# Norming row tiles one by one at the end of an output projection, with a longer tail for one stream

## The chip, the cores and the metric

The kernel runs on one core of a Trainium2 chip. The metric is the device time of one execution in microseconds (us). TensorE does the matmuls, VectorE (DVE) and ScalarE (ACT) the work on rows and columns, GpSimd (POOL) a few small operations, and SyncE (SP) issues most transfers from HBM.

## The reference

Two blocks run one after the other on 256 tokens of width 1024; the change is in the second. This has two layers, and it carries two streams, the latent tokens x and the context tokens xc, 256 tokens each. Each layer has three sub-layers: a feed-forward network, a mix of attentions and a Fourier transform, and another feed-forward network. In each of them the rows are normed and modulated, go through the sub-layer, and its output is normed and added back:

```python
def ffn_sublayer(h, m, sub, g_pre, g_post, w1, w2):
    shift, scale, gate = mods_of(m, sub)
    y = swiglu(modulate(rms_norm(h, g_pre[sub]), shift, scale), w1, w2)
    return h + MACARON_WEIGHT * gate * rms_norm(y, g_post[sub])
...
    o = jnp.concatenate([o_a, o_b, o_c], axis=-1) @ w_out
    x = x + gt * rms_norm(o, g_post[1])
    x = ffn_sublayer(x, mod, 2, g_pre, g_post, w_ffn_in[1], w_ffn_out[1])
```

In the last layer the context stream ends with the attention's keys and values: the last output projection of an attention and the last feed-forward network work on x alone.

## The kernel before

All matmuls run as three products of float32 parts: a matrix is split into a high half `h` (a cast on ScalarE, L175) and a low half `l` (a subtraction on VectorE, L176), and h·h, h·l and l·h are added up in PSUM. `wload` does it for weights: a transfer of 128 x 1024 into `wr` (4 buffers), then the split into `wh` and `wl` (3 buffers each).

`out_proj` (L1366 on) is the last step of every sub-layer: the product with the output weights, the norm of its rows, and the addition to `X[s][t]`. Rows come in tiles of 128: `t` is 0 or 1 within stream `s`. So `n` is 4 with two streams and 2 with one. The width of 1024 is done in two halves, `c` = 0 and 1. For each half the loop over weight tiles `u` does both or all four row tiles with each weight tile, but holds the last two weight tiles back (`rest`). With them the row tiles are completed two at a time and one after the other, so that the work on a finished tile runs beside the matmuls of the next one. With four tiles, part of an earlier weight tile is held back for tiles 2 and 3 as well (`split`).

The work on a finished row tile `i` of half 1: a Square on ScalarE whose sum is kept (L1411), the product with the gate into `tmp` (L1417, VectorE), the sum of the squares of both halves (L1419), a power of -1/2 on GpSimd (`rsqrt`, L204), and two updates of x, half by half (L1424).

If a sub-layer follows (`nxt`), its first step stands in here. `rows(s, t)` norms a tile's rows: two squares on ScalarE (L1326), their sum (L1328), a power on GpSimd, and one scaling (L1331) into `xn`. `cols(s)` then turns the normed rows of both tiles of a stream with 16 transposes on TensorE (L170), applies shift and scale on ScalarE (L1347) and splits the result into `hh` and `hl` on VectorE (L1350, L1351). Before, `rows` for both tiles of a stream follows the update of its second tile. With one stream `cols` comes right behind; with two, `cols(0)` is written behind the matmuls of tiles 2 and 3, and `cols(1)` is called by the next sub-layer's `first_units`, which also loads that sub-layer's first weights. With one stream all of these but the first are queued behind the first operations of `cols` (`issue_after`).

Five calls of `out_proj` have a `nxt`: the two feed-forward networks and the attention of layer 0 and the first feed-forward network of layer 1 with two streams, and the attention of layer 1 with one. The last feed-forward network has none. In layer 0 a generator (`mods_rows`) computes later modulations on VectorE in the background (L1188), a piece per weight load.

The order of the instructions on each engine is made by a scheduler, which takes what its own model of the times has ready, and of that what is written first. An engine then runs its instructions in that fixed order.

Of the kernel before, what the change touches and what calls it, by code (L numbers as in the profile page):

```python
# [157 lines left out]
class Build:  # L158
# [1207 lines left out]
    def out_proj(self, l, sub, streams, w, KT, lhs, weight, nxt, spare, yo=None, ahead=None):  # L1366

        nc = self.nc
        V, A, G = nc.vector, nc.scalar, nc.gpsimd
        g = self.gate(l, sub, streams)  # L1370
        tiles = [(s, t) for s in streams for t in range(2)]
        n, KU = len(tiles), KT // 2
        yo = self.yout() if yo is None else yo
        y = [spare[:, 0], spare[:, 1], yo[:, 0], yo[:, 1]]
        sq = self.us.tile([128, 2, 4], F32, name="sq", bufs=2)

        def load(u, *pool):
            h, lo = ahead.pop(0) if ahead else self.wload(w[:, 1024 * u : 1024 * u + 1024], 1024)
            return [(h[:, 512 * k :], lo[:, 512 * k :]) + lhs(2 * (u % KU) + k, *pool) for k in range(2)]

        def product(ps, i, k, parts):
            o = 256 * tiles[i][0] + 128 * tiles[i][1]
            h, lo, a, b = parts
            self.move(ps[i], h, lo, 1, k, KT, lambda _: (a[:, o : o + 128], b[:, o : o + 128]))

        for c in range(2):

            ps = [self.acc() if (c == 0 and i < 2) or (c and n == 4 and i) else self.bank() for i in range(n)]
            split = c and nxt and n == 4
            for u in range(KU - 2):  # L1390
                early = split and u == KU - 3
                parts = load(c * KU + u, *((self.pt, "pt", "pt") if early else ()))
                for k in range(2):
                    for i in range(2 if early else n):
                        product(ps, i, 2 * u + k, parts[k])

            rest = [p for u in range(KU - 2, KU) for p in load(c * KU + u)]
            if c and nxt:
                self.pre(*nxt)
            for i, (s, t) in enumerate(tiles):  # L1400
                if t == 0:
                    if split and s:
                        for k in range(2):
                            for j in (i, i + 1):
                                product(ps, j, KT - 6 + k, parts[k])
                    for j in (i, i + 1):
                        for k, r in enumerate(rest):
                            product(ps, j, KT - 4 + k, r)
                    if c and nxt and s:
                        self.cols(0)  # L1410
                A.activation(self.junk(), ps[i], AF.Square, accum_out=sq[:, c, i : i + 1])  # L1411
                half = slice(512 * c, 512 * c + 512)
                if c == 0:
                    V.tensor_tensor(out=y[i], in0=ps[i], in1=g[:, s, half], op=ALU.mult)
                    continue
                tmp = self.u2.tile([128, 512], F32, name="u2")
                V.tensor_tensor(out=tmp, in0=ps[i], in1=g[:, s, half], op=ALU.mult)  # L1417
                rs = self.us.tile([128, 1], F32, name="rso")
                V.scalar_tensor_tensor(out=rs, in0=sq[:, 0, i : i + 1], scalar=D * RMS_EPS, in1=sq[:, 1, i : i + 1],  # L1419
                                       op0=ALU.add, op1=ALU.add)  # L1420
                self.rsqrt(rs, rs, 1)
                for c2, part in enumerate((y[i], tmp)):
                    x = self.X[s][t][:, 512 * c2 : 512 * c2 + 512]
                    V.scalar_tensor_tensor(out=x, in0=part, scalar=rs, in1=x, op0=ALU.mult, op1=ALU.add)  # L1424
                if nxt and t:
                    for t2 in range(2):
                        self.rows(s, t2)
                    if n == 2:
                        self.cols(s)

    def first_units(self, n, streams, src):
# [403 lines left out]
```

## Time and profile before

| | |
|---|---|
| time, median of 3 runs | 2624.18 us (2622.79 to 2625.65) |
| the profiled execution | 2622.96 us |
| its span | 2621.1 us |
| TensorE matmuls busy | 2530.6 us (97%), 16658 instructions |
| VectorE busy | 1753.0 us (67%) |
| ScalarE busy | 1132.1 us (43%) |
| GpSimd busy | 183.7 us (7%) |
| read from HBM | 379.80 MB, 146 GB/s over the span |

A busy time is the sum over an engine's instructions. The span runs from the first to the last instruction of the profiled execution; the device time has 1.86 us around it. In the page's slices TensorE is busy to 90% or more in all but the first and the last.

### The profile page before, as it was taken

The page shows a single profiled execution, that of the slowest core. Times are in us where ns is not written, and L with a number is a line of the kernel's source. Part 1 is how long each engine was busy: PE and PEld are TensorE (multiplying, and loading weights), DVE is VectorE, ACT ScalarE, POOL GpSimd, SP SyncE. Part 2 cuts the span into 40 slices and gives each one's busy share as a digit, 9 for nine tenths or more (in the row PEclk, how much of TensorE's full clock was granted, in tenths as well). Part 3 has the DMA queues.
Part 4 walks back from the last instruction along what each step waited for, and adds up shares of the span by engine and source line. Part 5 has one row for each costly group of instructions (what it writes and reads, how often), then busy time and mean ns, then how long its engine had stood idle before and what let it go on. Part 6 is the DMA issues. An engine that isn't in the chain of part 4 may idle for free.

```text
span 2621.1 us, 42324 instructions
## 1 busy us (share of the span) xinstructions
PE 2530.6 (97%) x16658; PEld 2158.3 (82%) x16658; DVE 1753.0 (67%) x3102; ACT 1132.1 (43%) x1936; POOL 183.7 (7%) x219
## 2 busy tenths in 40 slices
PE   8999999999999999999999999999999999999998
PEld 7888999877899888887866778887788888866897
DVE  6988567797766785567777475556664445655656
ACT  5365445444545432233546342223432224555545
POOL 1121100112100000000112010000000000011000
PEclk9999999999999999999999999999999999999999
DMA  6334466545537564445441244444445543322565
GB/s 201 108 117 138 131 202 213 164 146 186 161 115 217 190 203 149 152 141 158 136 123 55 89 145 153 153 153 137 149 156 153 153 137 97 105 89 80 171 194 152
DMA packets 124711, 384.82 MB, mean 147 GB/s; under 512 B 28352, under 2 KB 32176, under 8 KB 124384
## 3 DMA queue, kind: packets, MB, share of 16 engines
q1 hardware_dynamic: 121504, 380.19, 47.3%
q8 instruction: 131, 2.15, 0.3%
q10 hardware_dynamic: 3008, 1.92, 0.2%
q14 instruction: 68, 0.56, 0.1%
HBM read 379.80 MB, written 2.26 MB: 146 GB/s over the span
## 4 chain that ended last, share of the span: by engine, by line
PE 74%; DVE 13%; DMA 6%; issue 4%; ACT 2%; POOL 1%; DVEq 0%; POOLq 0%; SPq 0%; ACTq 0%
PE ac L167 38%; PE rw L167 22%; PE sm L167 9%; DMA wr<-in_wmodT 5%; DVE wl L176 4%; PE md L167 3%; PE sm L170 2%; DVE br L816 2%; DVE prod L1188 1%; DMA wr<-in_win 1%; ACT wh L175 1%; POOL rs L204 1%; DVE blk L1351 0%; DVE br L1424 0%; PE rw L170 0%
## 5 line engine op out<-in xcount | busy, mean ns | idle before, releaser
L175 ACT CAST wh<-wr 128x1024 fp32r<-128x1024 f32 (+2 forms) x547 | 569.3, 1042 | 850.2 <-PE ac L167 375.8
L176 DVE TENSOR_TENSOR wl<-wr,wh 128x1024 fp32r<-128x1024 f32 (+2 forms) x547 | 665.1, 1217 | 239.4 <-ACT wh L175 233.9
L1188 DVE CUSTOM_DVE_ANT_0 prod<-wr,cr 128x1024 f32<-128x1024 f32 x208 | 254.4, 1223 | 305.8 <-DMA wr<-in_wmodT 304.7
L167 PE MATMUL rw<-blk,wh 128*128 128x512 f32 (+1 forms) x1600 | 423.3, 350 | 5.3 <-DVE blk L1350 4.7
L167 PE MATMUL ac<-blk,wh 128*128 128x512 f32 (+1 forms) x1552 | 410.4, 350 | 2.6 <-DVE blk L1350 1.8
L167 PE MATMUL ac<-xth,wh 128*128 128x256 f32 x1248 | 357.5, 287 | 7.2 <-ACT wh L175 5.2
L167 PE MATMUL ac<-xth,wl 128*128 128x256 f32 x1248 | 351.0, 281 | 2.7 <-DVE wl L176 2.6
L167 PE MATMUL ac<-xtl,wh 128*128 128x256 f32 x1248 | 350.0, 281 | 0.1
L167 PEld LDWEIGHTS rw<-blk,wh 128*128 128x128 f32 x1600 | 283.0, 189 | 46.5 <-DVE blk L1350 5.6
L167 PEld LDWEIGHTS ac<-blk,wh 128*128 128x128 f32 x1552 | 274.2, 189 | 42.2 <-DVE blk L1350 2.3
L167 PE MATMUL rw<-blk,wl 128*128 128x512 f32 (+1 forms) x800 | 279.2, 349 | 2.2 <-DVE wl L176 2.2
L167 PE MATMUL ac<-blk,wl 128*128 128x512 f32 (+1 forms) x776 | 271.0, 349 | 2.0 <-DVE wl L176 2.0
L167 PEld LDWEIGHTS ac<-xth,wh 128*128 128x128 f32 x1248 | 236.9, 190 | 17.7 <-issue 7.3
L167 PEld LDWEIGHTS ac<-xth,wl 128*128 128x128 f32 x1248 | 236.4, 190 | 6.1 <-DVE wl L176 4.7
L167 PEld LDWEIGHTS ac<-xtl,wh 128*128 128x128 f32 x1248 | 236.6, 190 | 2.5 <-issue 1.5
L175 ACT CAST ah<-blk 128x512 fp32r<-128x512 f32 (+1 forms) x170 | 95.8, 566 | 194.1 <-PE sm L167 99.7
L167 PEld LDWEIGHTS rw<-blk,wl 128*128 128x128 f32 x800 | 151.2, 189 | 22.4 <-DVE wl L176 3.1
L167 PEld LDWEIGHTS ac<-blk,wl 128*128 128x128 f32 x776 | 146.9, 189 | 21.7 <-DVE wl L176 2.6
L176 DVE TENSOR_TENSOR al<-blk,ah 128x512 fp32r<-128x512 f32 (+1 forms) x170 | 104.0, 620 | 62.2 <-ACT ah L175 62.0
L816 DVE SCALAR_TENSOR_TENSOR br<-hp,pv,br 128x256 f32<-128x256 f32 x240 | 114.1, 511 | 0.9
L167 PE MATMUL ac<-f,wh 128*128 128x256 f32 x640 | 114.1, 281 | 0.0
L167 PEld LDWEIGHTS ac<-f,wh 128*128 128x128 f32 x640 | 97.1, 188 | 1.1 <-issue 0.6
(440 smaller groups left out, 4136.9 us busy)
## 6 DMA issues: line engine op xcount, KB each, us to landing
wr<-in_w SPq DMA_DIRECT2D x264, 512.0 KB
wr<-in_win SPq DMA_DIRECT2D x187, 512.0 KB
wr<-in_wmodT SPq DMA_DIRECT2D x120, 512.0 KB
wr<-in_wo SPq DMA_DIRECT2D x32, 512.0 KB
wr<-in_wout SPq DMA_DIRECT2D x32, 512.0 KB
wr<-in_wmod SPq DMA_DIRECT2D x24, 512.0 KB
wr<-in_wkv SPq DMA_DIRECT2D x16, 512.0 KB
gate<-gd SPq DMA_DIRECT2D x10, 512.0 KB
```

Of the source, the lines that this page charges most:

```text
L167: self.nc.tensor.matmul(out, a, b, start=start, stop=stop, skip_group_check=True)
L170: self.nc.tensor.transpose(out, a, self.ident[:n, :n])
L175: nc.scalar.copy(h, src)
L176: (eng or nc.vector).tensor_tensor(out=l, in0=src, in1=h.bitcast(F32), op=ALU.subtract)
L204: self.nc.gpsimd.tensor_tensor(out=out, in0=in_, in1=self.mhalf[:p, :n], op=ALU.pow)
L816: V.scalar_tensor_tensor(out=acc, in0=hp[:, j : j + 256], scalar=w(j), in1=acc, op0=ALU.mult, op1=ALU.add)
L1188: V.tensor_tensor_reduce(out=self.prod, in0=raw, in1=self.cr[:, r], scale=1.0, scalar=0.0, op0=ALU.mult, op1=ALU.add, accum_out=m[:, g, r ...
```

## The change

With `nxt`, `rows` for a tile now follows that tile's own update, ahead of the work on the next tile, and no longer waits for the second tile of its stream. And with one stream, in the second half of the width, three weight tiles are held back instead of two, so that the two row tiles are completed with 18 matmuls each, one after the other, instead of 12. Nothing else changes: the same instructions on the same data.

```diff
--- before.py
+++ after.py
@@ -1387,14 +1387,16 @@
 
             ps = [self.acc() if (c == 0 and i < 2) or (c and n == 4 and i) else self.bank() for i in range(n)]
             split = c and nxt and n == 4
-            for u in range(KU - 2):
+
+            tail = 3 if c and nxt and n == 2 else 2
+            for u in range(KU - tail):
                 early = split and u == KU - 3
                 parts = load(c * KU + u, *((self.pt, "pt", "pt") if early else ()))
                 for k in range(2):
                     for i in range(2 if early else n):
                         product(ps, i, 2 * u + k, parts[k])
 
-            rest = [p for u in range(KU - 2, KU) for p in load(c * KU + u)]
+            rest = [p for u in range(KU - tail, KU) for p in load(c * KU + u)]
             if c and nxt:
                 self.pre(*nxt)
             for i, (s, t) in enumerate(tiles):
@@ -1405,7 +1407,7 @@
                                 product(ps, j, KT - 6 + k, parts[k])
                     for j in (i, i + 1):
                         for k, r in enumerate(rest):
-                            product(ps, j, KT - 4 + k, r)
+                            product(ps, j, KT - 2 * tail + k, r)
                     if c and nxt and s:
                         self.cols(0)
                 A.activation(self.junk(), ps[i], AF.Square, accum_out=sq[:, c, i : i + 1])
@@ -1422,10 +1424,9 @@
                 for c2, part in enumerate((y[i], tmp)):
                     x = self.X[s][t][:, 512 * c2 : 512 * c2 + 512]
                     V.scalar_tensor_tensor(out=x, in0=part, scalar=rs, in1=x, op0=ALU.mult, op1=ALU.add)
-                if nxt and t:
-                    for t2 in range(2):
-                        self.rows(s, t2)
-                    if n == 2:
+                if nxt:
+                    self.rows(s, t)
+                    if n == 2 and t:
                         self.cols(s)
 
     def first_units(self, n, streams, src):
```

## Rows read from the trace of the kernel before

**Rows 1.** Busy time by stage; columns: window, length, engines (instructions), clock, DMA share, GB/s.

```profile
1265.00:1298.00 33.00, 28.90 (x168) 24.95 (x166) 25.90 (x51) 17.02 (x40) 6.65 (x8) 0.95 0.43 118
1500.00:1535.00 35.00, 29.70 (x180) 25.36 (x179) 27.35 (x54) 18.45 (x43) 9.44 (x8) 1.00 0.43 136
1881.00:1914.00 33.00, 27.66 (x175) 23.91 (x174) 25.54 (x52) 18.86 (x43) 6.26 (x8) 1.00 0.40 127
2252.00:2285.00 33.00, 30.70 (x190) 27.23 (x189) 25.15 (x50) 18.76 (x43) 4.70 (x8) 0.95 0.36 91
2418.00:2440.00 22.00, 15.82 (x91) 13.54 (x91) 14.40 (x27) 12.28 (x25) 2.21 (x4) 0.84 0.37 118
```

**Rows 2.** Timeline, TensorE, one-stream end: start, duration, instruction, [idle before <-releaser].

```profile
2429.45 0.87 PE L170 MATMUL sm<-ident,u 128*128 128x128 f32 x3 [5.33 <-DVE rs L1328]
```

**Rows 3.** Chain that ended last, one-stream end: start, length, engine and line.

```profile
2413.24 8.18 PE sm L167 x36
...
2421.49 0.70 ACT junk L1411 x2
...
2426.40 1.42 DVE br L1424 x2
...
2428.55 0.75 DVE u L1331
...
2430.03 0.76 DVE u L1331
```

**Rows 4.** Timeline, ScalarE, one-stream end.

```profile
2418.71 1.05 ACT L175 CAST wh<-wr 128x1024 fp32r<-128x1024 f32 x1 [1.67 <-PE sm L167]
...
2424.21 0.60 ACT L1411 ACTIVATE junk<-sm 128x512 bf16<-128x512 f32 x1 [2.03 <-PE sm L167]
...
2427.25 0.63 ACT L1326 ACTIVATE junk<-br 128x512 bf16<-128x512 f32 x1 [0.84 <-DVE br L1424]
...
2428.54 0.19 ACT L1326 ACTIVATION_READ_ACCUMULATOR junk<-br 128x1 f32 x1
```

**Rows 5.** Timeline, VectorE, one-stream end.

```profile
2417.08 1.23 DVE L176 TENSOR_TENSOR wl<-wr,wh 128x1024 fp32r<-128x1024 f32 x1 [0.85 <-ACT wh L175]
...
2423.66 0.75 DVE L1424 SCALAR_TENSOR_TENSOR br<-blk,rso,br 128x512 f32<-128x512 f32 x1 [0.69 <-POOL rso L204]
```

**Rows 6.** Timeline, VectorE, third two-stream end.

```profile
1889.33 0.15 DVE L1328 SCALAR_TENSOR_TENSOR rs<-ss 128x1 f32<-128x1 f32 x1
1890.21 0.75 DVE L1331 TENSOR_SCALAR u<-br,rs 128x1024 f32<-128x1024 f32 x1 [0.73 <-POOL rs L204]
1890.88 1.22 DVE L176 TENSOR_TENSOR wl<-wr,wh 128x1024 fp32r<-128x1024 f32 x1
...
1892.89 0.75 DVE L1331 TENSOR_SCALAR u<-br,rs 128x1024 f32<-128x1024 f32 x1 [0.73 <-POOL rs L204]
```

**Rows 7.** Timeline, TensorE, first, second and fourth two-stream ends.

```profile
1280.34 1.64 PE L170 MATMUL sm<-ident,u 128*128 128x128 f32 x13 [1.61 <-DVE u L1331]
...
1516.20 1.65 PE L170 MATMUL sm<-ident,u 128*128 128x128 f32 x13 [1.15 <-DVE u L1331]
...
2267.72 0.39 PE L167 MATMUL rw<-blk,wh 128*128 128x256 f32 x1 [1.67 <-DVE blk L1350]
```

**Rows 8.** Timeline, TensorE, second half of the third end.

```profile
1905.87 0.38 PE L167 MATMUL ac<-blk,wl 128*128 128x256 f32 x1 [1.37 <-DVE wl L176]
```

**Rows 9.** Busy time in 2 us of the fourth end.

```profile
2270.00:2272.00 2.00, 2.00 (x11) 2.00 (x11) 2.00 (x7) 0.56 (x1) 0.00 (x0) 0.50 0.46 105
```

**Rows 10.** Timeline, ScalarE, third end.

```profile
1884.16 0.60 ACT L1411 ACTIVATE junk<-rw 128x512 bf16<-128x512 f32 x1 [2.09 <-PE rw L167]
...
1887.33 0.19 ACT L1326 ACTIVATION_READ_ACCUMULATOR junk<-br 128x1 f32 x1
```

**Rows 11.** Timeline, GpSimd, second and third end.

```profile
1512.41 1.46 POOL L204 TENSOR_TENSOR rs<-rs,mhalf 128x1 f32<-128x1 f32 x1 [1.60 <-DVE rs L1328]
...
1889.62 0.55 POOL L204 TENSOR_TENSOR rs<-rs,mhalf 128x1 f32<-128x1 f32 x1 [1.66 <-DVE rs L1328]
```

## The prediction

> **What bounds the kernel now.** I read the page first: TensorE is busy for 97% of the span, so a change that adds no arithmetic can only win back TensorE's idle time. Then I made a table by stage around the five places where this change acts, the ends of the output projections that norm rows for a next sub-layer. Four have two streams (four row tiles); one, in the last attention, has one stream (two tiles) [rows 1]. In these windows TensorE is idle for 4.1, 5.3, 5.3, 2.3 and 6.2 us (window less busy time), together 23.2 us or 0.9% of the span. That is the ceiling, and part of it belongs to the casts behind the norm, which stay.
>
> TensorE's timeline at the one-stream end shows one gap of 5.33 us, which ends when rows are normed [rows 2]. The chain of waits leads through it: ScalarE's square of the finished product, VectorE's product with the gate, a power on GpSimd, two updates of x, two squares; then, for each tile, a one-column sum, a power and the scaling [rows 3]. The two scalings start at 2428.55 and 2430.03, since tile 1's sum stands in VectorE's queue behind tile 0's scaling. That is what the change takes apart.
>
> **The change part by part.** No instruction is added or removed. In the one-stream tail 18 matmuls of each tile instead of 12 are done tile by tile, rows() moves up by one tile, and no DMA moves with it.
>
> *The one-stream end (once).* 36 matmuls of this tail take 8.18 us, 0.227 us each [rows 3]. With three held weight tiles, six more matmuls of tile 1 stand behind tile 0, so tile 0's product is complete 6 x 0.227 = 1.36 us earlier, and its Square moves from 2421.49 to about 2420.13. Tile 1 completes as before, its Square ready to run at 2424.21 [rows 4]. Tile 0's updates move from 2423.66 [rows 5] to 2422.30 and end at 2423.72 (1.42 us, [rows 3]). Its two squares then run from about 2423.15 to 2424.63: such a pair takes 1.48 us, as from 2427.25 to 2428.73 [rows 4]. They are written ahead of tile 1's Square now, which thus starts at 2424.63 and not at 2424.21: 0.42 us lost. Gained is that tile 1's sum no longer waits for tile 0's scaling, which ends at 2429.30 [rows 3]; its squares are read at 2428.73, so at most 0.57 us. The two nearly cancel: I take -0.1 us, with bounds -0.57 (tile 1's Square goes first) and +0.42 (only the loss stays). The gap of 5.33 us is a chain of tile 1 alone, from its own Square on, and more cover for tile 0 does not shorten that.
>
> The third held tile has two costs that I put at nothing. The last weight's low half is ready at 2417.08 + 1.23 = 2418.31 [rows 5]. Tile 0's 18 matmuls then end at 2413.24 + 8.18 - 1.36 = 2420.06 [rows 3], so they start some 0.2 us (the way of the last result) over 4.09 us earlier, at about 2415.8, and want this half after 13 of them, at about 2418.75. The cover is 0.4 us; without it TensorE stalls by what is missing, and tile 1's Square comes as much later. And the next sub-layer's first weight, whose cast now runs at 2418.71 in a free place of the weight buffer [rows 4], must wait until tile 1 has used the first held tile, to about 2421.3. Its cast (1.05 us) fits into ScalarE's pause before tile 0's squares, its split (1.23 us) into VectorE's pause after tile 0's updates (2423.7 to 2425), and it is needed only past the transposes, after 2431. Behind them are queued the squares of tile 0 and the gate product of tile 1, at most 0.4 us late. With this the bounds are -0.6 and +0.8 us.
>
> *The two-stream ends (four).* The products don't change here; only rows() moves. In VectorE's timeline of the third one, tile 0's sum follows tile 1's updates at 1889.33, the scaling starts 0.88 us later, at 1890.21, after 0.73 us of idle time, the next instruction at 1890.88, and tile 1's scaling at 1892.89 [rows 6]. Tile 0's norm thus takes 0.88 + 0.67 = 1.55 us of the queue between tile 1's updates and tile 1's sum. Moved up, its own work (0.07 + 0.67) still lies ahead of tile 1's last update, but the wait for its power is covered by tile 1's power and first update. Saved: 1.55 - 0.74 = 0.81 us per end. Does TensorE get it? In the first three ends it waits for a scaling, by 1.61 us in the first and 1.15 in the second, the least; in all four it then waits for a cast, by 1.67 us in the fourth [rows 7], and the casts stand in the same queue of VectorE behind the same waits. So I take 0.8 us each, -3.2 us in all. Bounds per end: 0 (a cast keeps its place behind a weight split that needs the same time) and -1.6 (tile 1's round trip to GpSimd is filled with other work too).
>
> *The second half of these ends (tiles 2 and 3).* Tile 2's norm moves ahead of tile 3's updates. TensorE doesn't wait for it there, but waits 1.37 us for a weight split in the third end [rows 8]; a scaling of 0.75 us put ahead of such a split would lengthen that. I take 0, with bounds -0.6 and +0.75 in three ends, +2.2 us.
>
> *The clock.* The granted clock is 0.50 (1.2 GHz) for a while after TensorE's idle stretch in the fourth end [rows 9]; the windows of the first and fourth ends average 0.95, those of the second and third, with more idle time, 1.00 and 1.00 [rows 1]. A mean of 0.95 over 33 us is 3.3 us at half speed, a loss of 1.65 us. A shift can take that away at two ends or bring it to two others: 0 taken, bounds -3.3 and +3.3.
>
> Sum: -0.1 - 3.2 = -3.3 us. The profiled execution, 2622.96 us (span 2621.1 and 1.86 around it), would become 2619.7; it lies 1.2 us under the median of 2624.18, against which I forecast 2624.18 - 3.3 = 2620.9 us.
>
> **The rivals.**
> *Written order in the queues, slower.* If ScalarE takes tile 0's two squares ahead of tile 1's Square at the two-stream ends too, that Square waits for tile 0's updates. In the third end tile 0's squares are read at 1887.52, and the Square that ran at 1884.16 starts then [rows 10]; tile 1's gate product comes behind tile 0's scaling, at 1887.52 + 0.88 + 0.67 = 1889.1. From there: 1.47 to the update (2422.19 to 2423.66), 1.42 for both, 0.91 until their squares are read (2427.82 to 2428.73), 0.88 and 0.75 [rows 3 to 6], so tile 1 is normed at 1894.5 instead of 1893.64: 0.9 us late, and 2.1 if the weight split of 1.22 us in that stretch still stands there. At the one-stream end the gate product starts at 2426.2 instead of 2425.08 (2423.66 + 1.42), less the 0.57: +0.6. In all +4.2 to +9.0, about 2631 us. It decides wherever tile 1's product is complete before tile 0's squares are done, so at all five ends. Against it: the trace is not in written order. The next sub-layer's first cast, written behind the whole projection, runs ahead of its last squares [rows 4], so what is ready goes first.
>
> *A stretched power, no change.* The power takes 0.55 us where VectorE idles for it, and 1.46 us where a weight split runs beside it [rows 11]. After the change VectorE works beside tile 0's power. If tile 1's are hit as well, 0.91 us per end are given back, more than the 0.81 gained: +0.4 - 0.1 us in all, 2624.5 us. For it speaks that a split is beside a power in the second end already; against it, that tile 1's powers keep their neighbours. The Trainium skill, "SBUF — State Buffer", section "Who interferes with whom", says that a VectorE instruction with two SBUF inputs and a GpSimd one that reads SBUF block each other for a whole instruction. By that rule a change that fills VectorE's waits pays with longer powers; the two rows agree with it.
>
> *A larger gain.* Both round trips are filled, and the clock stays up at the first and fourth ends: -6.4 - 0.1 - 3.3 = -9.8 us at most, about 2616 us with half of the clock's part. For it: waits of over 1.1 us for a scaling at three ends [rows 7]; against it, that the casts stay in the same queue.
>
> **How the numbers follow.** Forecast, -1 to -5.2 us: 0.58. No change, by stretched powers or because the casts keep their place: 0.17. Larger gain: 0.16. Written order: 0.09. 0.2% is 5.2 us, about what a measurement of this kernel can tell from no change. The forecast, but for a tail of 0.04 below, and the no-change case lie within it, the larger gain beyond it, written order beyond it in two cases of three: faster 0.20, same 0.74, slower 0.06. The range reaches into the larger gain, down to 2615.5, and over the no-change case with the bounds of the second halves, up to 2626.5; most of the slower rival and a tail of the larger gain stay outside.
>
> **What would show it.** Right: at the one-stream end tile 0's Square 4.1 to 4.5 us ahead of tile 1's instead of 2.7, and the gap still near 5 us; at the two-stream ends tile 0's scaling ahead of tile 1's last update, and waits for a scaling shorter by some 0.8 us. Wrong: tile 1's Square behind tile 0's squares at the two-stream ends (written order); powers over 1 us in tile 1's chain (stretched); the last weight late, as a wait of TensorE for a split inside the one-stream tail; a gap well under 5 us there, which would mean that I missed what sets it.

## The result: 0.57% slower

| | before | after |
|---|---|---|
| time, median of 5 runs on one chip | 2625.65 us (2622.79 to 2631.76) | 2643.23 us (2635.35 to 2644.3) |
| ratio, 95% interval | | 1.0057 (1.0034 to 1.008) |
| the profiled execution | 2622.96 us | 2641.94 us |
| its span | 2621.1 us | 2640.1 us |
| mean granted clock of TensorE | 0.992 | 0.984 |

The forecast was 3.3 us less, within 2615.5 to 2626.5. The ratio, which is not the quotient of the two medians (1.0067), says some 15 us more, with an interval of about 9 to 21 us. The sign was wrong and the range missed the time.

Of the profiled execution after the change, the page's busy times:

```profile
PE 2541.4 (96%) x16658; PEld 2175.0 (82%) x16658; DVE 1754.6 (66%) x3102; ACT 1133.8 (43%) x1936; POOL 180.0 (7%) x219
```

The number of matmuls is the same, and VectorE and ScalarE work as long as before. TensorE is busy 10.8 us longer (2530.6 before) and idle 8.2 us longer (span less busy time: 90.5 before, 98.7 now). Both show in one group of instructions, the transposes of `cols`; its idle time grows by more than the whole, since other waits fall away (those for the casts of `cols`, 6.5 us before). Columns: busy us, mean ns | idle just before them, and what ended it. First after, then before.

```profile
L170 PE MATMUL sm<-ident,u 128*128 128x128 f32 x416 | 73.7, 315 | 38.7 <-DVE u L1331 33.6
```

```profile
L170 PE MATMUL sm<-ident,u 128*128 128x128 f32 x416 | 65.1, 288 | 19.5 <-DVE u L1331 11.5 <-DVE rs L1328 5.3 <-ACT u L1347 1.3
```

TensorE now waits 33.6 us for scalings of rows (L1331) instead of 16.8 (11.5 + 5.3), and the same transposes take 8.6 us longer, since the clock is lower when they run.

**Where it happens: the order of two queues.** In the code after, the Square of `out_proj` is L1413, the gate product L1419, the updates of x L1426; `rows` keeps its lines. ScalarE's timeline in the third two-stream end, after, answers [rows 10]:

```profile
1890.63 0.60 ACT L1413 ACTIVATE junk<-sm 128x512 bf16<-128x512 f32 x1 [4.09 <-PE sm L167]
...
1894.97 0.63 ACT L1326 ACTIVATE junk<-br 128x512 bf16<-128x512 f32 x1 [3.65 <-DVE br L1426]
...
1895.72 0.63 ACT L1326 ACTIVATE junk<-br 128x512 bf16<-128x512 f32 x1
...
1896.48 0.60 ACT L1413 ACTIVATE junk<-rw 128x512 bf16<-128x512 f32 x1
```

Tile 1's Square (`rw`) follows tile 0's (`sm`) by 5.85 us. Before it followed by 2.78 us (1881.38 below and 1884.16, [rows 10]), when TensorE finished the product. Now it stands behind tile 0's two squares of `rows`. ScalarE idles 3.65 us ahead of these, though tile 1's product is ready from about 1893.4 on (2.78 us after tile 0's Square). The second half has the same order, and there it costs more. ScalarE before, then after:

```profile
1881.38 0.60 ACT L1411 ACTIVATE junk<-sm 128x512 bf16<-128x512 f32 x1 [4.09 <-PE sm L167]
...
1892.33 0.60 ACT L1411 ACTIVATE junk<-rw 128x512 bf16<-128x512 f32 x1 [0.36 <-PE rw L167]
```

```profile
1912.11 0.63 ACT L1326 ACTIVATE junk<-xc 128x512 bf16<-128x512 f32 x1 [2.13 <-DVE xc L1426]
...
1913.63 0.60 ACT L1413 ACTIVATE junk<-rw 128x512 bf16<-128x512 f32 x1
```

Before, tile 3's Square ran when its product was done (1892.33). After, TensorE starts the last matmul of that product at 1901.08, and the Square comes at 1913.63, some 12 us later: it stands behind tile 2's two squares, and these behind tile 2's updates, which VectorE does only after the casts of `cols(0)`. VectorE in the third end, after (answers [rows 6]):

```profile
1896.48 0.16 DVE L1328 SCALAR_TENSOR_TENSOR rs<-ss 128x1 f32<-128x1 f32 x1 [0.94 <-ACT junk L1326]
1897.37 0.75 DVE L1331 TENSOR_SCALAR u<-br,rs 128x1024 f32<-128x1024 f32 x1 [0.73 <-POOL rs L204]
1898.04 0.68 DVE L1419 TENSOR_TENSOR u<-rw,gate 128x512 f32<-128x512 f32 x1
...
1903.60 0.75 DVE L1331 TENSOR_SCALAR u<-br,rs 128x1024 f32<-128x1024 f32 x1 [0.73 <-POOL rs L204]
...
1914.67 0.75 DVE L1331 TENSOR_SCALAR u<-xc,rs 128x1024 f32<-128x1024 f32 x1 [0.73 <-POOL rs L204]
1915.34 0.68 DVE L1419 TENSOR_TENSOR u<-rw,gate 128x512 f32<-128x512 f32 x1
...
1920.18 0.75 DVE L1331 TENSOR_SCALAR u<-xc,rs 128x1024 f32<-128x1024 f32 x1 [0.56 <-POOL rs L204]
```

Tile 1's gate product starts only when tile 0 has been scaled (1898.04 behind 1897.37), and in the second half tile 3's behind tile 2's (1915.34 behind 1914.67). The two tiles of a stream are now worked on one after the other, round trips to ScalarE and GpSimd included, where before they overlapped: from tile 2's scaling to tile 3's it takes 5.51 us, before 1.55 us. TensorE's timeline, after, second halves of the four two-stream ends (tiles 2 and 3):

```profile
1300.71 2.61 PE L170 MATMUL sm<-ident,u 128*128 128x128 f32 x11 [3.58 <-DVE u L1331]
...
1537.67 3.03 PE L170 MATMUL sm<-ident,u 128*128 128x128 f32 x13 [4.56 <-DVE u L1331]
...
1920.99 2.10 PE L170 MATMUL sm<-ident,u 128*128 128x128 f32 x11 [3.82 <-DVE u L1331]
...
2294.62 1.64 PE L170 MATMUL sm<-ident,u 128*128 128x128 f32 x11 [1.40 <-DVE u L1331]
```

Adding up all waits of TensorE in its timeline over 42 us at each of the five ends gives:

| | first halves | second halves | one-stream end | sum |
|---|---|---|---|---|
| before | 12.9 | 4.0 | 6.1 | 23.0 |
| after | 14.6 | 13.4 | 6.5 | 34.5 |

**The clock.** Busy time in 40 us at each end, after (columns as in [rows 1], the clock third from the end):

```profile
1266.00:1306.00 40.00, 31.17 (x179) 28.05 (x178) 29.43 (x57) 18.87 (x43) 4.77 (x8) 0.87 0.45 126
1502.00:1542.00 40.00, 32.31 (x176) 29.31 (x175) 30.28 (x58) 18.86 (x43) 8.07 (x8) 0.84 0.43 132
1888.00:1928.00 40.00, 33.35 (x197) 30.20 (x196) 27.48 (x57) 18.87 (x43) 6.09 (x8) 0.91 0.37 119
2261.00:2301.00 40.00, 35.24 (x206) 31.18 (x205) 26.92 (x51) 18.89 (x43) 4.39 (x8) 0.91 0.37 93
2434.00:2474.00 40.00, 33.45 (x235) 31.18 (x234) 26.10 (x42) 20.90 (x38) 2.21 (x4) 0.87 0.52 155
```

Before, such windows average 0.96, 1.00, 1.00, 0.96 and 0.91. One minus the clock, times 40 us, adds up to 6.8 us before and 24 us after. In 2 us each, in the third end after:

```profile
1905.00:1907.00 2.00, 2.00 (x12) 2.00 (x11) 2.00 (x6) 1.71 (x4) 1.00 (x1) 0.50 0.26 33
...
1921.00:1923.00 2.00, 2.00 (x12) 1.87 (x13) 1.04 (x6) 1.65 (x4) 0.00 (x0) 0.64 0.73 279
1923.00:1925.00 2.00, 2.00 (x11) 2.00 (x11) 1.93 (x5) 2.00 (x5) 0.00 (x0) 0.51 0.04 16
```

TensorE comes back from each of its two long waits (to 1904.41 and to 1920.99), and soon after works at 0.50 and 0.51 of full speed (1.2 GHz) in 2 us. In the third end before, with waits of at most 1.77 us, the clock stayed at 1.00. So in this end each long wait is paid a second time. That isn't so of every wait, and its length alone doesn't decide: in the fourth end before, the clock fell behind waits of at most 1.67 us [rows 7 and 9], and in the first end after, nine transposes ran at 1.00 (1281 to 1283) behind a wait of 2.76 us; the clock fell in the next wait, of 2.50 us:

```profile
1281.16 1.20 PE L170 MATMUL sm<-ident,u 128*128 128x128 f32 x9 [2.76 <-DVE u L1331]
```

8.6 of the 10.8 us of busy time are in the transposes; of the rest it can't be told, since single executions differ by as much (below).

**The one-stream end** has the same order. ScalarE, VectorE and TensorE, after:

```profile
2437.52 0.60 ACT L1413 ACTIVATE junk<-sm 128x512 bf16<-128x512 f32 x1 [3.09 <-PE sm L167]
...
2441.29 0.63 ACT L1326 ACTIVATE junk<-br 128x512 bf16<-128x512 f32 x1
...
2442.05 0.60 ACT L1413 ACTIVATE junk<-sm 128x512 bf16<-128x512 f32 x1
```

```profile
2442.97 0.75 DVE L1331 TENSOR_SCALAR u<-br,rs 128x1024 f32<-128x1024 f32 x1 [0.66 <-POOL rs L204]
2443.64 0.68 DVE L1419 TENSOR_TENSOR u<-sm,gate 128x512 f32<-128x512 f32 x1
```

```profile
2443.87 0.98 PE L170 MATMUL sm<-ident,u 128*128 128x128 f32 x3 [2.37 <-DVE u L1331]
...
2449.03 2.61 PE L170 MATMUL sm<-ident,u 128*128 128x128 f32 x11 [4.18 <-DVE u L1331]
```

The gap of [rows 2] (5.33 us, and 0.52 behind it for tile 1's scaling) is two gaps now, together 6.55 us.

### The profile page after: what moved, and what is told of

It reads as the page before. It is cut to its first block, busy times and chain, and to the rows that moved or that the text cites. A ratio compares the mean times of both kernels' runs of the same rounds, so it can differ in the third digit from the quotient of the medians.

```text
span 2640.1 us, 42322 instructions
## 1 busy us (share of the span) xinstructions
PE 2541.4 (96%) x16658; PEld 2175.0 (82%) x16658; DVE 1754.6 (66%) x3102; ACT 1133.8 (43%) x1936; POOL 180.0 (7%) x219
## 4 chain that ended last, share of the span: by engine, by line
PE 79%; DVE 11%; DMA 3%; issue 3%; ACT 2%; POOL 2%; DVEq 0%; SPq 0%; POOLq 0%; ACTq 0%
PE ac L167 40%; PE rw L167 24%; PE sm L167 10%; DVE wl L176 3%; PE md L167 3%; PE sm L170 2%; DVE br L816 2%; DMA wr<-in_wmodT 2%; DMA wr<-in_win 1%; DVE prod L1188 1%; ACT wh L175 1%; POOL rs L204 1%; ACT junk L1326 1%; DVE u L1331 1%; DVE blk L1351 0%
## 5 line engine op out<-in xcount | busy, mean ns | idle before, releaser
L167 PEld LDWEIGHTS rw<-blk,wl 128*128 128x128 f32 x800 | 153.1, 191 | 20.3 <-DVE wl L176 0.8
L170 PE MATMUL sm<-ident,u 128*128 128x128 f32 x416 | 73.7, 315 | 38.7 <-DVE u L1331 33.6
```

The costliest lines, as they stand in the source:

```text
L167: self.nc.tensor.matmul(out, a, b, start=start, stop=stop, skip_group_check=True)
L170: self.nc.tensor.transpose(out, a, self.ident[:n, :n])
```

## The experiments

Every ratio is against the kernel before on the same chip (its median 2617.03 to 2617.42 us there). The theory was that the written order in ScalarE's queue makes the loss; the rivals, that norming tile by tile does as such, or that the longer tail does.

**The two parts apart.** First only `rows` moved, then only the tail of three:

```diff
-                if nxt and t:
-                    for t2 in range(2):
-                        self.rows(s, t2)
-                    if n == 2:
+                if nxt:
+                    self.rows(s, t)
+                    if n == 2 and t:
```

> Only rows() moves, at all five ends; the tail of the one-stream end holds two weight tiles as before. Theory 1 (queue order: the second tile's Square and gate product stand behind the first tile's norm): nearly the whole loss stays, +14 to +18 us over the kernel before, since four of the five ends are as in the changed kernel. Theory 2 (the longer tail, with the next sub-layer's first weight behind it, is what costs): at most +5 us.

```diff
+            tail = 3 if c and nxt and n == 2 else 2
-            for u in range(KU - 2):
+            for u in range(KU - tail):
```

> Only the one-stream tail is longer; rows() stays behind the second tile everywhere. Theory 1: within 1 us of the kernel before; tile 0's Square comes 1.36 us earlier and the gap on TensorE stays near 5.3 us. Theory 2: +5 us or more.

Moving `rows` alone: 2630.84 us, ratio 1.0054 (1.0037 to 1.0072), about +14 us. The tail alone: 2615.61 us, 0.9989 (0.9976 to 1.0002). So the loss comes with `rows`, and none is to be seen from the tail. The transposes in the kernel with `rows` alone take 73.7 us, with 40.9 us of idle time before them, as after the change. With the tail alone the one-stream gap stays, which TensorE's timeline shows:

```profile
2418.59 0.87 PE L170 MATMUL sm<-ident,u 128*128 128x128 f32 x3 [5.29 <-DVE rs L1328]
2419.98 2.56 PE L170 MATMUL sm<-ident,u 128*128 128x128 f32 x11 [0.52 <-DVE u L1331]
```

5.29 us against 5.33: that gap is the chain of tile 1, and more cover for tile 0 doesn't shorten it, as the prediction said.

**First halves or second halves.** `rows` tile by tile only in stream 0, then only in stream 1, of the two-stream ends:

```diff
-                if nxt and t:
+                if nxt and (n == 4 and s == 0):
+                    self.rows(s, t)
+                elif nxt and t:
```

> rows() moves at the four two-stream ends for tiles 0 and 1 only. In the changed kernel's trace the way from tile 0's Square to the first transposes of the second stream is 2.3 us longer in the sum of the four ends. Theory 1, with the loss where nothing covers the chain: 0 to +4 us. If both halves lose alike (theory 1 without cover): +7 to +9 us.

```diff
-                if nxt and t:
+                if nxt and (n == 4 and s == 1):
+                    self.rows(s, t)
+                elif nxt and t:
```

> rows() moves at the four two-stream ends for tiles 2 and 3 only. Theory 1, with the loss where nothing covers the chain: +11 to +16 us, with waits of TensorE for the fourth tile's scaling of 1.4 to 4.6 us at each end, as in the changed kernel, and half-speed clock behind them. If both halves lose alike: +7 to +9 us.

First halves: 2619.08 us, 1.0008 (0.9996 to 1.0019), about +2 us and no loss that is clear of noise. Second halves: 2634.12 us, 1.0058 (1.0041 to 1.0076), about +15 us, as much as the whole change. TensorE in the second half of the third end with `rows` moved there alone:

```profile
1907.47 0.53 PE L170 MATMUL sm<-ident,u 128*128 128x128 f32 x3 [0.26 <-DVE u L1331]
...
1912.76 2.60 PE L170 MATMUL sm<-ident,u 128*128 128x128 f32 x11 [4.65 <-DVE u L1331]
```

It does tile 2's transposes and then waits 4.65 us: what covers the norm of stream 1 are the next sub-layer's first matmuls on stream 0, and they have run out before tile 3 is normed. In the first halves the longer wait for a scaling takes the place of others: in the third end after the change it is 2.83 us, where before there were 1.36 for the scaling and 1.77 for a cast.

**Is it the queue order, or norming tile by tile as such?** The whole change, but with both Squares of a stream written ahead of the rest (`gated` is gate product, sum and power of one tile, `update` its two updates):

```diff
+                square(i)
+                square(i + 1)
+                update(i, *gated(i))
+                self.rows(s, 0)
+                update(i + 1, *gated(i + 1))
+                self.rows(s, 1)
```

> The whole change (rows() tile by tile, longer one-stream tail), but the Squares of both products of a stream are written ahead of the first tile's updates and rows(). Theory 1, in the form that ScalarE's order alone is the cause: the loss is gone and the gain of the prediction's first sum appears, -1 to -5 us against the kernel before. Theory 3 (it is VectorE's queue, where rows() still is written ahead of the second tile's gate product): +7 us or more.

2616.68 us, 1.0005 (0.9992 to 1.0019): the loss is gone, and no gain is to be seen, where 1 to 5 us were expected. ScalarE, VectorE and TensorE in the third end of this kernel:

```profile
1878.00 0.60 ACT L1433 ACTIVATE junk<-sm 128x512 bf16<-128x512 f32 x1 [4.09 <-PE sm L167]
...
1880.78 0.60 ACT L1433 ACTIVATE junk<-rw 128x512 bf16<-128x512 f32 x1 [2.09 <-PE rw L167]
```

```profile
1886.03 0.76 DVE L1342 TENSOR_SCALAR u<-br,rs 128x1024 f32<-128x1024 f32 x1 [0.44 <-POOL rs L204]
...
1888.71 0.75 DVE L1342 TENSOR_SCALAR u<-br,rs 128x1024 f32<-128x1024 f32 x1 [0.73 <-POOL rs L204]
```

```profile
1889.52 1.65 PE L170 MATMUL sm<-ident,u 128*128 128x128 f32 x13 [0.56 <-DVE u L1342]
...
1893.62 0.39 PE L167 MATMUL ac<-blk,wh 128*128 128x256 f32 x1 [1.77 <-DVE blk L1361]
...
1901.85 0.52 PE L170 MATMUL sm<-ident,u 128*128 128x128 f32 x3 [1.53 <-DVE u L1342]
```

The Squares are 2.78 us apart again, and tile 3's runs when its product is done (1888.95). VectorE's gate product of tile 1, though written behind `rows` of tile 0 as after the change, now runs ahead of tile 0's scaling (1882.62 and 1886.03), so the order written on VectorE is not the cause. Tile 1's scaling starts 10.71 us after tile 0's Square; before it was 11.51 (1892.89 less 1881.38). That is the 0.8 us of the forecast, and TensorE's wait for it falls by as much, from 1.36 to 0.56 us. The wait for the cast stays at 1.77. In the second half TensorE then waits 1.53 us for tile 2's scaling, which before it didn't: tile 2's transposes are queued ahead of matmuls that are still to do. The first end shows the same 1.53 us.

The same with a tail of two, and with `rows(s, 0)` kept behind the second Square by a dependence as well:

```diff
+                last = square(i + 1)
...
+                with self.tc.issue_after(last.ins):
+                    self.rows(s, 0)
```

> As the run with both Squares first, but with the one-stream tail of two weight tiles of the kernel before. Theory 1: 0 to -4 us; the distance to the run with the longer tail is what that tail is worth, within 2 us.

2615.52 us, 0.9997 (0.9985 to 1.0009). A difference by the length of the tail is not to be seen here either.

**Only ScalarE's order.** The kernel before, with nothing moved but the two squares of `rows(s, 0)`: they are written behind tile 0's update, ahead of tile 1's Square. Sum, power and scaling stay written behind tile 1's update.

```diff
+                if nxt and t == 0:
+                    first = self.rows_squares(s, 0)
                 if nxt and t:
-                    for t2 in range(2):
-                        self.rows(s, t2)
+                    self.rows(s, 0, first)
+                    self.rows(s, 1)
```

> The kernel before, with one thing moved: the first tile's two squares of rows() are written right behind that tile's update, so ahead of the second tile's Square; sum, power and scaling of both tiles stay written behind the second tile's updates, the tail has two weight tiles. Theory 1: the whole loss of the run that moves only rows(), +12 to +17 us. Theory 3: within 4 us of the kernel before.

2634.34 us, 1.0072 (1.0053 to 1.009), about +19 us: the whole loss, and a little more than the 12 to 17 us expected. ScalarE, VectorE and TensorE in its third end:

```profile
1879.78 0.60 ACT L1419 ACTIVATE junk<-sm 128x512 bf16<-128x512 f32 x1 [4.09 <-PE sm L167]
...
1884.66 0.63 ACT L1326 ACTIVATE junk<-br 128x512 bf16<-128x512 f32 x1
...
1885.42 0.60 ACT L1419 ACTIVATE junk<-rw 128x512 bf16<-128x512 f32 x1
```

```profile
1886.31 0.75 DVE L1339 TENSOR_SCALAR u<-br,rs 128x1024 f32<-128x1024 f32 x1 [0.73 <-POOL rs L204]
1886.98 0.68 DVE L1425 TENSOR_TENSOR u<-rw,gate 128x512 f32<-128x512 f32 x1
```

```profile
1893.36 3.04 PE L170 MATMUL sm<-ident,u 128*128 128x128 f32 x13 [2.63 <-DVE u L1339]
...
1909.97 2.61 PE L170 MATMUL sm<-ident,u 128*128 128x128 f32 x11 [3.83 <-DVE u L1339]
```

VectorE's scaling of tile 0 isn't written ahead of tile 1's gate product here, and yet it runs ahead of it. Where VectorE idles before a gate product, the trace names the tile's Square as what ended the wait (before, at 2422.21: 1.19 us for L1411), so a late Square takes the gate product with it. That the scheduler therefore had the scaling ready first is inferred; no run shows its model. Two squares of 0.63 us each, put ahead of one other instruction in each place, on an engine that is busy 43% of the time, reproduce it all.

**The one-stream end alone.** The whole change with `n == 2`, two-stream ends as before:

```diff
-                if nxt and t:
+                if nxt and (n == 2):
+                    self.rows(s, t)
+                elif nxt and t:
```

> The whole change at the one-stream end (longer tail and rows() tile by tile), the four two-stream ends as in the kernel before. From the changed kernel's trace this end costs 1.1 us over the kernel before: 0 to +2 us. The prediction's sum for it was -0.1 us.

2617.29 us, 1.0003 (0.9987 to 1.0018). TensorE waits 2.37 and 4.33 us there, together 6.70 where the tail alone has 6.03 (5.29, 0.52 and 0.22 for a cast). A loss of 0.7 us in that place is seen in the trace, not in the time.

**Is there anything to win?** Both Squares first, and `rows` tile by tile only in the first halves and at the one-stream end; then the same with the updates of tiles 2 and 3 queued behind the first casts of `cols(0)`, which TensorE waits for:

```diff
+                if n == 2 or s == 0:
+                    self.rows(s, 0)
+                update(i + 1, *gated(i + 1))
+                if n == 4 and s:
+                    self.rows(s, 0)
```

> Both Squares first; rows() tile by tile only for tiles 0 and 1 and at the one-stream end (with the longer tail), and for tiles 2 and 3 as in the kernel before. In the run with both Squares first, TensorE won 0.8 us before the first transposes of the third end and lost 1.53 us again where it now waits for tile 2's scaling. If that is where the gain went: no wait of that kind at the second halves, the four first halves shorter by 0.5 to 1 us each, -1 to -4 us in all. If the gain is not there to be had: within 1 us of the kernel before.

```diff
+                if s:
+                    g0, g1 = gated(i), gated(i + 1)
+                    with self.tc.issue_after(self.mark[1]):
+                        update(i, *g0)
+                        update(i + 1, *g1)
```

> As the run with first halves only, and VectorE's updates of tiles 2 and 3 are queued behind the first casts of the transposed rows. Those casts then no longer stand behind an update and its wait for the power (0.73 + 0.67 us): TensorE's wait for the first cast, 1.4 to 1.8 us at three ends, falls by 0.7 to 1.4 us. -3 to -7 us against the kernel before; if the weight split and the background product in front of the casts set the wait, no more than the run with first halves only.

2615.84 us, 0.999 (0.9977 to 1.0002), and 2615.85 us, 0.9992 (0.9978 to 1.0006), where the second expectation had 3 to 7 us less. All waits at the five ends come to 22.2 and 20.3 us, 23.0 before. In the last one a wait for a weight split takes the place of those for casts, as TensorE's timeline of the third end shows:

```profile
1889.23 0.39 PE L167 MATMUL ac<-blk,wh 128*128 128x256 f32 x1 [0.95 <-DVE blk L1350]
...
1897.97 0.38 PE L167 MATMUL ac<-blk,wl 128*128 128x256 f32 x1 [2.07 <-DVE wl L176]
```

The cast's wait falls from 1.77 to 0.95 us, and 2.07 us go to a split that had 1.37 [rows 8]. If either kernel is faster than the one before, it is by less than these runs can tell.

## Why the prediction was wrong

**The step that failed** is the choice between the forecast and the rival "written order in the queues". That rival had the mechanism, at all five ends, and got a chance of 0.09. The argument against it was that the trace is not in written order, since a cast written late runs ahead of squares written early [rows 4], "so what is ready goes first". But the order is made before the run by the scheduler's own model, and what counts is what that model has ready. That a cast went ahead shows only that the scheduler can move things; it says nothing of tile 0's squares against tile 1's Square. In the runs these squares go first wherever they are written first, though at the third end tile 1's product was done before them (1893.4 against 1894.97); no run shows the model's times, so why it has them ready first stays open. The prediction was also at odds with itself: for the one-stream end its sum took the written order (tile 1's Square behind tile 0's squares, 0.42 us late), for the two-stream ends the opposite. The order in the kernel that was to come could not be read from the trace, and so the case deserved far more than 0.09.

**The terms that failed** in the sum are two. The first halves were to give 3.2 us; their waits grew by 1.7 us instead (12.9 to 14.6), and the run with the first halves alone lay between 1 us faster and 5 us slower. The larger one is the second half of the two-stream ends: "I take 0, with bounds -0.6 and +0.75 in three ends". Measured: waits of 13.4 instead of 4.0 us over the four, +9.4. The term looked only at tile 2's scaling of 0.75 us put ahead of a split, not at tile 3's chain behind it, whose Square came some 12 us after its product.

**The rival's price** was right in its delays. In the third end it put tile 1's scaling 0.9 to 2.1 us late; measured from tile 0's Square, it starts after 12.97 us instead of 11.51, 1.46 late. At the one-stream end it came to +0.6; measured +0.5 in the table of waits and +0.7 in the kernel with that end alone. It was wrong in what they cost: its 4.2 to 9.0 us were for the first halves and the one-stream end, and the change in these places alone costs about 2 and 1 us, neither clear of noise. It left out the second halves, which cost about 15 us alone, and the clock. The right mechanism was priced in the wrong place.

**The clock** was taken at 0 with bounds of 3.3 us, since it could fall at two more ends and recover at two. It fell at all five: 17 us more of missing clock at the ends. Part of that lies in idle time and costs nothing. Weighted with TensorE's busy time in windows of 2 us it is 18.6 us after and 5.0 before, 13.6 us of work lost, which is an upper bound, since a busy stretch needn't be bound by the clock. The missing clock at the ends separates the kernels: 20.5 to 23.9 us for the four with the loss (after, `rows` alone, second halves alone, the two squares alone), 6.8 to 11.9 for the other eight, that before included. TensorE's whole busy time doesn't: it is 2535.8 to 2541.4 us for the four and 2527.9 to 2541.5 for the eight, so single executions differ elsewhere by as much as the 10.8 us. The group of the 416 transposes does: 72.0 to 73.7 us busy and 37.9 to 40.9 idle before them for the four, 65.1 to 68.7 and 14.8 to 24.8 for the eight. How the 15 us split between waits and clock stays open by a few us.

**The stretched power**, the other rival, is in the trace but didn't decide it. A power in tile 1's chain in the third end is hit, as it feared; GpSimd's timeline, after:

```profile
1898.93 1.40 POOL L204 TENSOR_TENSOR rso<-rso,mhalf 128x1 f32<-128x1 f32 x1 [1.60 <-DVE rso L1421]
```

A split runs on VectorE beside it (1.22 us from 1898.70), and it takes 1.40 us instead of 0.55. By the rule of the Trainium skill that the prediction cited ("SBUF — State Buffer", "Who interferes with whom") it should, and the trace agrees. VectorE then idles 0.44 us for it, less than a third of tile 1's 1.46 us. Over this end two powers are over 1 us after the change (1.40 and 1.40) and two before (1.58 and 1.40). With both Squares first powers of 0.92, 1.58 and 0.92 us stand there, and nothing is lost.

**What held.** The 0.8 us per first half is there once the order is right (10.71 instead of 11.51, a wait of 0.56 instead of 1.36), though no gain in time could be measured, and part is given back later (the 1.53 us). The forecast's 3.2 us for four such ends lie outside the interval of the kernel with both Squares first (at most 2.1 us faster) and inside that of the one that keeps the second halves as before (at most 6.0). At the one-stream end tile 0's Square leads by 4.53 us (forecast 4.1 to 4.5), tile 1's starts 0.44 us late (forecast 0.42; the product is done 18 matmuls of 0.227 us behind tile 0's, so this Square could start at 2437.52 + 4.09 = 2441.61, and starts at 2442.05). The last weight makes TensorE wait nowhere in the tail, and no cost of the longer tail alone was measured. The gap there is tile 1's own chain, which no version shortened below some 5.1 us.

## What to carry to other kernels

When work on one tile is moved ahead of work on the next, look at every engine that the moved work touches, and ask whether its first instruction there now stands ahead of an instruction that the next tile's chain begins with; an engine that is 43% busy can still be the one whose order makes the loss. Issue the first short step of all tiles before the second step of any. And price a delay at the place with the least cover: here the same reordering cost little where the new wait took the place of others, and nearly all of the loss where TensorE had no work left beside it.

## What the runs showed of the hardware

A wait of TensorE of a few us could be paid twice: in the third end its granted clock was 0.50 from 1905 to 1907, behind a wait of 2.83 us that ended at 1904.41, and 0.51 from 1923 to 1925, behind one of 3.82 us that ended at 1920.99. The 13 transposes behind the first took 3.00 us instead of 1.64. Not every such wait was: behind one of 2.76 us in the first end the clock was still 1.00. Over the kernel the same 416 transposes took 73.7 instead of 65.1 us.
